# Summing the modulation over partitions with TensorE from the whole tile, at a later place in its order

## The chip, the cores and the metric

The kernel runs on one core of a Trainium2 chip. The metric is the time of one execution on the device in microseconds; less is better. PE is TensorE (matrix products), PEld its loading of weights, DVE VectorE, ACT ScalarE, POOL GpSimd, and SP SyncE, which issues the transfers.

## The reference, cut to what matters

Two blocks of two layers each, one sequence of 256 tokens of width 1024, all in fp32. The first block has a gated linear attention, an mLSTM and two mixtures of 16 experts. The second block is a transformer whose norms and residuals are modulated by a vector `c` (`ada`):

```
c_act = silu(c)                                    # 1 x 1024
for l in range(2):
    ada = c_act @ w_ada[l] + b_ada[l]              # 1 x 6144
    sh1, sc1, gt1, sh2, sc2, gt2 = split(ada, 6)
    h = rms(x, g_mix[l]) * (1 + sc1) + sh1
    ...                                            # two attentions, gates, mixed
    x = x + gt1 * (mixed @ w_out[l])
    h2 = rms(x, g_mlp[l]) * (1 + sc2) + sh2
    x = x + gt2 * (square(relu(h2 @ w_ff1[l])) @ w_ff2[l])
```

`ada` hangs on the input `c` alone, so it can be computed at any time before the norm that needs it. It is a product of one row with a 1024 x 6144 matrix for each layer.

## The kernel before

One program computes everything. Each engine has its own queue, worked in order; the order in which the program emits instructions is the order of every queue. The main line (dense products on PE) is emitted by plain functions (`dense`, `dense_T`, `out_proj`, `block_qk`), and after each step of it `B.tick()` lets the side jobs, written as generators, emit their next piece. A `Clock` keeps an estimated time for every engine and tile, from fixed costs; the choice between two engines (`AV`, `VG`, `VG2`) and the `calm` waits of side jobs go by these estimates. Weights of the dense products come as chunks of 128 x 1024 that are split into a high half (`hi`, by ACT or DVE) and a low half (`lo`, by DVE or POOL), two chunks ahead of their use.

`ada_cols` is the side job for `ada`. It takes the 12 column blocks j of 512 columns of each layer l, 24 blocks in all, (l, j), number n; each in four quarters q of 256 rows. A quarter is a transfer of 128 x 2 x 512, on ACT a product of its first half with a scalar per partition, and on DVE a product with the second half added. Quarters 1 to 3 are added to the tile of quarter 0, `acc`, by DVE or POOL. After the fourth, `acc` holds 128 x 512 terms still to be summed over the 128 partitions. Before the change DVE does the larger part of it: a transposition of all 32 x 32 squares, and a sum over 32 elements into `part` (128 x 4 x 4). PE finishes: four matmuls with 128 x 32 of `part` and the constant `c_fold` fold the four partition groups, each for its own 32 of the 128 output partitions. A matmul of fp32 shows as two records in the trace.

PE's step is a hook. `hooks` is a list of functions that wait for a good place in PE's order: the start of each dense product, its middle where `drained` is set, and in `out_proj` each chunk while the modulation of the second norm isn't there. A hook is taken there if `bool(hooks)` says that its input is ready on the planner's clock. Where something needs the result at once, `ada_need` (before the first norm of a layer (l, 3), before the second (l, 9)) and `unhook` (while side jobs are drained) take it without asking. The sum goes into the first columns of the PSUM tile that the dense product will use next, and ACT or DVE copies it out as `raw`.

Three tiles of 128 x 512 (`ada_T`) hold the quarters; `ada_used` says which are taken. Block n has its accumulator in tile n mod 3. Block numbers from 4 on are paced by `start` along the weight chunks. While the experts' weights stream, free tiles of the three serve as room for them (`ada_room`).

Of the kernel before, what the change touches and what calls it, by code (L numbers as in the profile page):

```python
# [26 lines left out]
F32 = mybir.dt.float32  # L27
# [4 lines left out]
OP = mybir.AluOpType  # L32
AX = mybir.AxisListType

P = 128
# [192 lines left out]
def tile_model(ctx: ExitStack, tc: tile.TileContext, I, out, stages=None, h_in=None):  # L228
    nc = tc.nc
    clock = Clock()  # L230
    PE, V, A, G = [Timed(clock, e, n) for e, n in
                   ((nc.tensor, "PE"), (nc.vector, "V"), (nc.scalar, "A"), (nc.gpsimd, "G"))]
# [8 lines left out]
    const = ctx.enter_context(tc.tile_pool(name="const", bufs=1))  # L241
# [163 lines left out]
    def kp_view(W, r0, rows, n0, n):  # L405
        return W[r0:r0 + rows, n0:n0 + n].rearrange("(k p) n -> p k n", p=P)
# [146 lines left out]
    class Hooks:  # L553
# [5 lines left out]
        def __bool__(self):  # L559
            if not self.fs:  # L560
                return False
            t = clock.t
            return max(clock.last(self.fs[0][1], False), min(t["A"], t["V"]) - 0.6) < t["PE"]

        def append(self, f, ap):
            self.fs.append((f, clock.span(ap)))
# [4 lines left out]
    hooks = Hooks()  # L571
# [204 lines left out]
    def gla():  # L776
# [23 lines left out]
        def load_ng(nb):  # L800
            ngs[nb] = bcast_row(ph, I["gla_norm_g"][:, nb * 512:(nb + 1) * 512], "row", 512)
        load_ng(0)
        small_loads()
        glr = early.tile([17, T], F32, name="glr")
        S.pump()
# [177 lines left out]
        if "l0" in stages:  # L983
            B.push(ada_cols(), side=True)
# [854 lines left out]
    ada_T, ada_used = [], {}  # L1839
# [8 lines left out]
    def ada_cols():  # L1848

        todo = [(l, j, q) for l in range(2) if f"l{l}" in stages for j in range(12) for q in range(4)]  # L1850
        ws = {}

        def load(i):
            if i < len(todo) and i not in ws and not ada_stop:
                l, j, q = todo[i]
                ada_open[0] += 1
                w = clock.slot("ada_w", 2, ada.tile([P, 2, 512], F32, name="ada_w", tag="ada_w", bufs=2))
                SP.dma_start(w, kp_view(I["w_ada_2"][l], q * 256, 256, j * 512, 512))
                ws[i] = w

        first = {g: next((i for i, (u, _) in enumerate(S.chunks) if S.units[u][3] == g), 0) for g in ("l0", "l1")}
        NB = (4, 10, 16, 22, 24)
        CB = [first["l0"] - 30, first["l0"] + 36, first["l1"] - 24, first["l1"] + 40, first["l1"] + 90]

        def start(x):
            i = max(j for j in range(4) if x >= NB[j])
            return CB[i] + (CB[i + 1] - CB[i]) * (x - NB[i]) / (NB[i + 1] - NB[i])

        load(0)
        load(1)  # L1870
        yield 14
        ada_T.extend(ada.tile([P, 512], F32, name="ada_t", tag=tag, bufs=n) for tag, n in
              (("ada_acc", 1), ("ada_t", 2), ("ada_t", 2)))
        acc = None
        for i, (l, j, q) in enumerate(todo):
            n = i // 4
            ada_at[0] = lambda: (load(i), load(i + 1))
            while i not in ws:
                load(i)
                load(i + 1)  # L1880
                yield 6 if i in ws else 1
            while n >= 4 and S.chunk_at < start(n + q / 4):
                yield
            while q == 1 and len(hooks.fs) > 1:
                yield
            w = ws[i]
            ada_used[n, q] = (n + (0, 2, 1, 2)[q]) % 3
            t = ada_T[ada_used[n, q]]
            if n >= 4:
                yield from calm("A", w)  # L1890
            A.activation(t, w[:, 0], AF.Copy, scale=ccol[:, 2 * q:2 * q + 1])
            if n >= 4:
                yield from calm("V", t)
            else:
                yield
            V.scalar_tensor_tensor(t, w[:, 1], ccol[:, 2 * q + 1:2 * q + 2], t, op0=OP.mult, op1=OP.add)
            ada_open[0] -= 1
            load(i + 2)
            if q:
                if n >= 4:  # L1900
                    yield from calm("G", t)
                else:
                    yield 1
                VG2.tensor_tensor(acc, acc, t, op=OP.add)
                if q < 3:
                    del ada_used[n, q]
            else:
                acc = t
                if n < 4:
                    yield 1  # L1910
            if q < 3:
                yield
                continue
            if n >= 4:
                yield from calm("V", acc)
            else:
                yield
            part = small.tile([P, 4, 4], F32, name="part", bufs=3)
            V.transpose(t, acc)
            if n >= 4:  # L1920
                yield from calm("V")
            V.tensor_reduce(part.rearrange("p k r -> p (k r)"), t.rearrange("p (b i) -> p b i", i=32), axis=AX.X,
                            op=OP.add)
            del ada_used[n, 0], ada_used[n, 3]

            def reduce(ps, l=l, j=j, part=part):
                for r in range(4):
                    PE.matmul(ps[32 * r:32 * r + 32, 0:4], c_fold, part[:, :, r], start=True, stop=True,
                              skip_group_check=True)
                k = slice(4 * j, 4 * j + 4)  # L1930
                raw = small.tile([P, 4], F32, name="raw", bufs=2)
                AV.copy(raw, ps[:, 0:4])
                VG2.tensor_tensor(adac[:, l, k], raw, bada[:, l, k], op=OP.add)
                if j % 6 == 3:

                    w = j // 6
                    V.tensor_copy(mod[:, l, w, 1], adac[:, l, 24 * w:24 * w + 8])
                    V.scalar_tensor_tensor(mod[:, l, w, 0], adac[:, l, 24 * w + 8:24 * w + 16], 1.0,
                                           gcol[:, l * 2 + w], op0=OP.add, op1=OP.mult)
                ada_done.add((l, j))  # L1940
            hooks.append(reduce, part)
            yield

    def calm(e, *aps):
        for _ in range(10):
            t = max([clock.t[e]] + [clock.last(clock.span(a), False, e) for a in aps])
            if t <= clock.t["PE"] + 0.9:
                return
            yield
# [472 lines left out]
    c_ident = ident  # L2422
# [7 lines left out]
                SP.dma_start(h[a * 64:a * 64 + 64, mt], rows[2 * mt + a])  # L2430
    n_kept = _OFFS[4][0]
    cst = const.tile([P, n_kept - P], F32, name="cst")
    c_fold = const.tile([P, 32], F32, name="fold")
    c_ones, c_iota, c_earl = [cst[:, o - P:o - P + n] for o, n in _OFFS[1:4]]
    mhalf = const.tile([P, 16], F32, name="mhalf")
    G.memset(mhalf, -0.5)
# [20 lines left out]

    def small_loads():
        ld = SP.dma_start
        V.tensor_reduce(c_fold, c_ident.rearrange("p (b m) -> p m b", m=32), axis=AX.X, op=OP.add)  # L2460
        ld(cst, I["cst"][:, P:n_kept])
        ld(rwg[:, 0], I["router_w"].rearrange("(k p) n -> p k n", p=P))
        for a, n in enumerate(("ln_g", "ln_b")):
            ld(lnpk[:, a], I[n][:, 0].rearrange("l (p k) -> p l k", k=8))
        ld(gatew, I["mlstm_w_in"][0][:, 4096:4104].rearrange("(k p) n -> p k n", p=P))
        for a in range(2):
            ld(bg[32 * a:32 * a + 4], I["mlstm_b_gates"][0, 4 * a:4 * a + 4].unsqueeze(1))
        ld(crow[0:64], I["mlstm_conv_w"][0].rearrange("j (f p) -> (j f) p", p=P))
        ld(crow[64:80], I["mlstm_conv_b"][0].rearrange("(f p) -> f p", p=P))
        ld(cb16.rearrange("p a b -> p (a b)"), I["cst"][:, _OFFS[4][0]:_OFFS[4][0] + 2 * P])  # L2470
# [82 lines left out]
    small = ctx.enter_context(sm_cm)  # L2553
# [21 lines left out]
    if first:  # L2575
        with tc.tile_pool(name="ring_b", bufs=RB) as rb, tc.tile_pool(name="rt", bufs=1) as rp, \
# [3 lines left out]
            if "gla" not in stages:  # L2580
                S.pump()
                small_loads()
# [6 lines left out]
            for i, s in enumerate(first):  # L2589
                nxt = (first + second)[i + 1] if i + 1 < len(first + second) else None  # L2590
                with tc.tile_pool(name="ph_" + s, bufs=1) as ph:
# [8 lines left out]
                    else:  # L2600
                        l = int(s[-1])
# [20 lines left out]
    else:  # L2622
        S.pump()
        small_loads()
        for _ in setup():
            pass
        B.push(ada_cols(), side=True)
    if second and not first:
        xin = rms_in(int(second[0][1]), 0)
# [34 lines left out]
```

## Time and profile before

| | |
|---|---|
| Time, median of 3 runs (lowest to highest) | 1734.81 us (1733.33 to 1739.93) |
| The profiled execution: time / span | 1734.7 us / 1732.9 us |
| Mean granted clock of TensorE | 0.953 |
| Instructions | 22647 |
| Busy: PE / PEld / DVE / ACT / POOL | 91% / 66% / 64% / 33% / 23% |
| Read from HBM | 419.77 MB, 243 GB/s over the span |

The span is the time from the first to the last instruction of the profiled execution. The second block's first layer begins near 845 us; its attention takes until about 1100, its MLP until about 1300, and the second layer the rest. The MLP of the first layer is where most of the second layer's modulation is computed. An idle time is put down to the event that ended it.

### The profile page before, as it was taken

The page shows a single profiled execution, that of the slowest core. Times are in us where ns is not written, and L with a number is a line of the kernel's source. Part 1 is how long each engine was busy: PE and PEld are TensorE (multiplying, and loading weights), DVE is VectorE, ACT ScalarE, POOL GpSimd, SP SyncE. Part 2 cuts the span into 40 slices and gives each one's busy share as a digit, 9 for nine tenths or more (in the row PEclk, how much of TensorE's full clock was granted, in tenths as well). Part 3 has the DMA queues.
Part 4 walks back from the last instruction along what each step waited for, and adds up shares of the span by engine and source line. Part 5 has one row for each costly group of instructions (what it writes and reads, how often), then busy time and mean ns, then how long its engine had stood idle before and what let it go on. Part 6 is the DMA issues. An engine that isn't in the chain of part 4 may idle for free.

```text
span 1732.9 us, 22647 instructions
## 1 busy us (share of the span) xinstructions
PE 1576.5 (91%) x8772; PEld 1136.3 (66%) x8774; DVE 1112.8 (64%) x1728; ACT 574.2 (33%) x973; POOL 395.3 (23%) x256
## 2 busy tenths in 40 slices
PE   7998999898998799989788998888998889989997
PEld 5865444336776544433466897778986679878996
DVE  4876113106887611121498979898889987779875
ACT  5223111105543211201344453533434544352210
POOL 1232000001333100000364324432125531222110
PEclk9998999898999899999998999999998999999999
DMA  9746999999755589999653676577764446547651
GB/s 321 284 149 229 360 392 411 391 360 238 240 190 194 198 322 373 409 406 387 208 179 110 196 202 221 171 250 257 250 240 152 158 138 179 191 137 241 194 180 41
DMA packets 165770, 422.43 MB, mean 244 GB/s; under 512 B 13017, under 2 KB 14193, under 8 KB 154642
## 3 DMA queue, kind: packets, MB, share of 16 engines
q1 hardware_dynamic: 165458, 420.75, 69.7%
q8 instruction: 73, 1.20, 0.3%
q14 instruction: 47, 0.39, 0.1%
q0 software_dynamic: 192, 0.10, 0.0%
HBM read 419.77 MB, written 1.05 MB: 243 GB/s over the span
## 4 chain that ended last, share of the span: by engine, by line
PE 27%; DVE 12%; issue 6%; ACT 2%; POOL 2%; DMA 1%; DVEq 0%; POOLq 0%; ACTq 0%
PE mm L175 16%; PE acc L175 7%; DVE ada_t L175 3%; DVE lo L175 2%; POOL lo L175 2%; PE sb L175 1%; DVE xs L175 1%; DMA ada_w<-in_w_ada 1%; DVE ro L175 1%; DVE rt L175 1%; ACT pa L175 1%; ACT hi L175 1%; DVE h L175 1%; DVE mx L175 1%; DVE hss L175 1%
## 5 line engine op out<-in xcount | busy, mean ns | idle before, releaser
L175 POOL TENSOR_TENSOR lo<-w,hi 128x1024 fp32r<-128x1024 f32 x104 | 264.4, 2548 | 505.7 <-ACT hi L175 495.9
L175 DVE TENSOR_TENSOR lo<-w,hi 128x1024 fp32r<-128x1024 f32 x204 | 261.4, 1287 | 21.2 <-ACT hi L175 15.3
L175 ACT CAST hi<-w 128x1024 fp32r<-128x1024 f32 x207 | 214.6, 1050 | 146.9 <-PE mm L175 99.9
L175 PE MATMUL mm<-hi,X_H 128*128 128x512 f32 x512 | 221.1, 432 | 29.8 <-ACT X_H L175 15.6
L175 PE MATMUL mm<-lo,X_H 128*128 128x512 f32 x512 | 210.5, 411 | 3.5 <-DVE lo L175 3.2
L175 PE MATMUL mm<-X_H,hi 128*128 128x256 f32 x704 | 206.0, 293 | 1.6 <-ACT raw L175 1.1
L175 PE MATMUL mm<-hi,X_L 128*128 128x512 f32 x512 | 197.4, 409 | 4.8 <-DVE X_L L175 4.7
L175 PE MATMUL mm<-X_L,hi 128*128 128x256 f32 x704 | 201.5, 286 | 0.0
L175 PE MATMUL mm<-X_H,lo 128*128 128x256 f32 x704 | 201.3, 286 | 0.0
L175 PE MATMUL up<-w,X 128*64 128x512 f32 x672 | 194.0, 599 | 0.8 <-ACT X L175 0.8
L175 PEld LDWEIGHTS mm<-hi,X_H 128*128 128x128 f32 x512 | 102.7, 201 | 61.5 <-issue 21.2
L175 PEld LDWEIGHTS mm<-X_H,hi 128*128 128x128 f32 x704 | 136.8, 194 | 4.0 <-ACT raw L175 1.3
L175 PEld LDWEIGHTS mm<-X_L,hi 128*128 128x128 f32 x704 | 137.0, 195 | 0.4
L175 PEld LDWEIGHTS mm<-X_H,lo 128*128 128x128 f32 x704 | 136.8, 194 | 0.0
L175 DVE SCALAR_TENSOR_TENSOR y<-dn,gsl,y 128x512 fp32r<-128x512 f32 x32 | 24.0, 751 | 162.0 <-ACT y L175 162.0
L175 POOL TENSOR_TENSOR ln_rs<-ln_rs,mhalf 128x1 f32<-128x1 f32 x8 | 4.9, 614 | 515.5 <-DVE ln_rs L175 515.5
L175 PEld LDWEIGHTS up<-w,X 128*64 128x64 f32 x672 | 58.7, 138 | 96.8 <-issue 93.0
L175 PEld LDWEIGHTS mm<-hi,X_L 128*128 128x128 f32 x512 | 100.7, 198 | 31.3 <-DVE X_L L175 8.5
L175 PEld LDWEIGHTS mm<-lo,X_H 128*128 128x128 f32 x512 | 102.8, 201 | 24.8 <-DVE lo L175 5.8
L175 PE MATMUL up<-wh,X 128*64 128x512 f32 x336 | 116.2, 604 | 0.0
L175 PE MATMUL dn<-w,hTt 128*64 128x512 f32 x336 | 105.3, 631 | 2.1 <-ACT hTt L175 2.1
L175 DVE TENSOR_TENSOR hb<-sa,up 128x512 f32<-128x512 f32 x16 | 11.0, 687 | 141.1 <-PE up L175 141.1
(412 smaller groups left out, 2953.2 us busy)
## 6 DMA issues: line engine op xcount, KB each, us to landing
w<-in_moe_w SPq DMA_DIRECT2D x126, 1024.0 KB, 9.8
w<-in_w_ff SPq DMA_DIRECT2D x64, 1024.0 KB, 5.5
wh<-in_moe_w SPq DMA_DIRECT2D x124, 512.0 KB, 11.5
ada_w<-in_w_ada SPq DMA_DIRECT2D x96, 512.0 KB, 4.2
w<-in_w_in SPq DMA_DIRECT2D x40, 1024.0 KB, 5.5
w<-in_mlstm_w_in SPq DMA_DIRECT2D x16, 1024.0 KB, 19.9
w<-in_gla_w_in SPq DMA_DIRECT2D x12, 1024.0 KB, 9.8
w<-in_w_out SPq DMA_DIRECT2D x8, 1024.0 KB, 6.1
```

What stands on the lines that cost most here:

```text
L175: r = f(*args, **kw)
```

## The change

DVE's transposition and sum go, with `part` and `c_fold`. PE sums each 128 x 128 quarter of `acc` over the partitions itself: the tile's columns are the weights, a column of ones moves, and the result is one column of 128 for each of the four. So four matmuls with 128 x 128 weights replace four with 128 x 32. The hook is taken at a place where the tile has been ready for 5 us on the planner's clock, unless it is taken without asking. `acc` stays taken until PE's sum is emitted; so the tiles of the quarters are dealt out in another order, and a wait of the job changes: before, the second quarter waited while more than one hook was open, now the third waits until the block before it has been summed.

```
-            return max(clock.last(self.fs[0][1], False), min(t["A"], t["V"]) - 0.6) < t["PE"]
+            return max(clock.last(self.fs[0][1], False) + 5.0, min(t["A"], t["V"]) - 0.6) < t["PE"]
...
-            while q == 1 and len(hooks.fs) > 1:
+            while (n - 1, 0) in ada_used and q == 2:
                 yield
             w = ws[i]
-            ada_used[n, q] = (n + (0, 2, 1, 2)[q]) % 3
+            ada_used[n, q] = (n + (0, 1, 2, 1)[q]) % 3
...
-            part = small.tile([P, 4, 4], F32, name="part", bufs=3)
-            V.transpose(t, acc)
-            if n >= 4:
-                yield from calm("V")
-            V.tensor_reduce(part.rearrange("p k r -> p (k r)"), t.rearrange("p (b i) -> p b i", i=32), axis=AX.X,
-                            op=OP.add)
-            del ada_used[n, 0], ada_used[n, 3]
-
-            def reduce(ps, l=l, j=j, part=part):
-                for r in range(4):
-                    PE.matmul(ps[32 * r:32 * r + 32, 0:4], c_fold, part[:, :, r], start=True, stop=True,
+            del ada_used[n, 3]
+
+            def reduce(ps, l=l, j=j, n=n, acc=acc):
+                for f in range(4):
+                    PE.matmul(ps[:, f:f + 1], acc[:, f * P:(f + 1) * P], c_ones[:, 0:1], start=True, stop=True,
                               skip_group_check=True)
+                del ada_used[n, 0]
...
-            hooks.append(reduce, part)
+            hooks.append(reduce, acc)
...
-    c_fold = const.tile([P, 32], F32, name="fold")
...
-        V.tensor_reduce(c_fold, c_ident.rearrange("p (b m) -> p m b", m=32), axis=AX.X, op=OP.add)
```

## Rows read from the trace of the kernel before

**Rows 1.** The page, busy time, share of the span and instructions of each engine.

```profile
PE 1576.5 (91%) x8772; PEld 1136.3 (66%) x8774; DVE 1112.8 (64%) x1728; ACT 574.2 (33%) x973; POOL 395.3 (23%) x256
```

**Rows 2.** Busy time by stretch: us, busy us of PE, PEld, DVE, ACT, POOL, PEclk, DMA share.

```profile
845.00:1100.00 255.00, 218.04 (x1336) 183.25 (x1338) 221.79 (x361) 115.99 (x234) 108.98 (x75) 0.93 0.55 176
1100.00:1205.00 105.00, 94.18 (x611) 85.34 (x610) 93.15 (x102) 46.41 (x68) 34.59 (x13) 0.93 0.74 249
1205.00:1300.00 95.00, 92.92 (x564) 81.79 (x562) 83.47 (x96) 36.23 (x48) 20.73 (x9) 1.00 0.71 240
```

**Rows 3.** Tile views of ada_t and part: duration ns min/median/max, first and last start us.

```profile
L175 DVE STREAM_TRANSPOSE ada_t<-ada_t x24: 696/711/715, 98.9 to 1620.5; 128x512 f32<-128x512 f32 x24
...
L175 DVE TENSOR_REDUCE part<-ada_t x24: 677/686/689, 99.7 to 1621.3; 128x16 f32<-128x512 f32 x24
```

**Rows 4.** Order of time on PE around one reduction: start us, us, what.

```profile
977.90 0.28 PE L175 MATMUL mm<-X_H,lo 128*128 128x256 f32 x1
978.11 0.25 PE L175 MATMUL mm<-part,fold 128*32 128x4 f32 x8
978.29 0.39 PE L175 MATMUL mm<-X_H,hi 128*128 128x256 f32 x1
978.51 0.28 PE L175 MATMUL mm<-X_L,hi 128*128 128x256 f32 x1
```

**Rows 5.** Order of time on PE, narrow matmuls with a full weight tile.

```profile
34.30 0.39 PE L175 MATMUL mm<-lo,X_H 128*128 128x512 f32 x1
34.52 1.84 PE L175 MATMUL dps<-cg,rg 128*128 128x4 f32 x16
36.23 0.47 PE L175 MATMUL mm<-hi,X_H 128*128 128x512 f32 x1
36.54 0.39 PE L175 MATMUL mm<-lo,X_H 128*128 128x512 f32 x1
```

**Rows 6.** Order of time on PE, the same weight width with 128 columns moving.

```profile
1261.61 1.95 PE L175 MATMUL adar<-ident,adac 128*128 128x128 f32 x16
1263.49 0.25 PE L175 MATMUL mm<-part,fold 128*32 128x4 f32 x8
```

**Rows 7.** Order of time on PE: the four reductions with an idle time before them.

```profile
532.16 0.25 PE L175 MATMUL bgp<-part,fold 128*32 128x4 f32 x8 [3.22 <-DVE part L175]
...
1139.23 0.24 PE L175 MATMUL bgp<-part,fold 128*32 128x4 f32 x8 [2.02 <-DVE part L175]
...
1160.69 0.28 PE L175 MATMUL mm<-part,fold 128*32 128x4 f32 x8 [4.27 <-DVE part L175]
...
1196.49 0.29 PE L175 MATMUL bgp<-part,fold 128*32 128x4 f32 x8 [3.45 <-DVE part L175]
```

**Rows 8.** Busy time by stretch behind two of these (PEclk is the granted clock).

```profile
1160.70:1165.20 4.50, 4.50 (x28) 4.48 (x29) 3.94 (x6) 1.82 (x3) 0.78 (x1) 0.50 1.03 382
...
1196.50:1202.90 6.40, 6.40 (x37) 6.38 (x38) 3.02 (x4) 2.61 (x4) 0.00 (x0) 0.50 0.88 288
```

**Rows 9.** Order of time on DVE behind the third of these idle times.

```profile
1162.03 1.22 DVE L175 TENSOR_TENSOR lo<-w,hi 128x1024 fp32r<-128x1024 f32 x1
```

**Rows 10.** Order of time on DVE and PE: waits of PE behind a reduction.

```profile
880.84 0.69 DVE L175 TENSOR_REDUCE part<-ada_t 128x16 f32<-128x512 f32 x1
...
887.52 0.77 PE L175 MATMUL mm<-hi,X_H 128*128 128x512 f32 x1 [4.02 <-DVE xs L175]
...
1337.26 0.76 PE L175 MATMUL mm<-hi,X_H 128*128 128x512 f32 x1 [3.45 <-DVE xs L175]
```

**Rows 11.** Order of time on DVE, the last quarter of block (0, 9).

```profile
1067.36 0.75 DVE L175 SCALAR_TENSOR_TENSOR ada_t<-ada_w,ccol,ada_t 128x512 f32<-128x512 f32 x1
...
1069.15 2.89 DVE L175 TENSOR_TENSOR ada_t<-ada_t 128x512 f32<-128x512 f32 x1
```

**Rows 12.** Order of time on PE: the reductions of blocks (0, 8) and (0, 9).

```profile
1055.00 0.24 PE L175 MATMUL mm<-part,fold 128*32 128x4 f32 x8
...
1073.63 0.24 PE L175 MATMUL bgp<-part,fold 128*32 128x4 f32 x8
```

## Prediction, made before the result was known

> **What bounds the kernel now.** Read the page's busy times first [rows 1]: PE is busy for 91% of the span, DVE for 64%. So PE idles for 1732.9 - 1576.5 = 156.4 us in all, and whatever the change does must either add to PE's work or take from those 156 us. The changed sums run along the whole kernel but belong to the second block, so the stretches come next [rows 2]. In the first attention stretch (845 to 1100) DVE is busy for 221.8 of 255 us and PE for 218.0: both are near their limit, and PE often waits for DVE. In the first half of the MLP (1100 to 1205) DVE has 93.2 of 105 us, PE 94.2, at a granted clock of 0.93. From 1205 to 1300 PE has 92.9 of 95 us: there, work taken from DVE buys nothing and work given to PE is paid in full.
>
> Then the sums themselves. Each of the 24 column blocks ends with a transposition and a reduction on DVE, 0.71 and 0.69 us [rows 3], together 24 x 1.40 = 33.6 us. PE then folds in eight records (four matmuls, two passes each). Last, PE in order of time: four of the 24 folds have an idle time before them that ended with DVE's reduction: 3.22 + 2.02 + 4.27 + 3.45 = 12.96 us [rows 7]. Behind the third and the fourth PE runs 4.5 and 6.4 us at a granted clock of 0.50, which is the 1.2 GHz level, where it had been idle just before [rows 8]. The same work at 2.4 GHz would have taken about half of these 10.9 us, so up to 5.4 us; matmuls bound by other things halve less, and I take 5.0.
>
> **What the change costs on PE.** A fold now takes little, because its weight tiles are 32 columns wide: eight records within 0.18 us (978.11 to 978.29). What it delays is more: from the matmul before it to the second behind it 0.61 us pass (977.90 to 978.51) where two usual steps of 0.12 us would make 0.24 [rows 4], so 0.37 us. The new matmuls load 128 x 128 of the tile as weights and move one column. Nothing in the trace moves one column, but 16 records with full weights and 4 columns take 1.71 us (34.52 to 36.23), 0.107 each; from the matmul before to the second behind 2.24 us pass where two steps of 0.23 make 0.46, so 16 records delay by 1.78 [rows 5]. With 128 columns moving a record takes 1.88 / 16 = 0.117 us [rows 6]. From 128 columns to 4 the step falls only by a tenth, so the weights set it, and one column will not be cheaper to speak of. Eight records then cost 8 x 0.107 = 0.86 and delay by 0.86 + 0.07 = 0.93. The difference per block is 0.93 - 0.37 = 0.56 at the least, and 0.86 - 0.18 = 0.68 if the edges cost as much as the fold's; I take 0.60, or 24 x 0.60 = 14.4 us in all. The lower bound, should the loads hide, is nothing.
>
> Here a rule bears on the sum. Rows 5 show 0.107 us per narrow record [rows 5]. The Trainium skill, TensorE: Matmul & The Clock Gate, section Back-to-back issue gap, gives streams of matmuls with up to 64 columns a gap of about 25 ns, and by that the eight records would cost no more than the fold does; the section LDWEIGHTS of the same page lets a load take its columns divided by 1.2 in ns, 107 for 128 columns, and by that the sum stands as above. The trace agrees with the second for full weights, and with 0.18 / 8 = 0.023 us for narrow ones it is near the first. The first is a rival below.
>
> Not every block pays. In two places PE goes from the fold straight into a wait for DVE's xs: the idle time before 887.52 begins at 883.50, that before 1337.26 at 1333.81 [rows 10]. What PE does there longer lies within these 4.02 and 3.45 us. The fold at 1055.00 [rows 12] also comes shortly before a wait. So 21 x 0.60 = 12.6 us are exposed; bounds 10 (more blocks hidden, 18 x 0.56) and 16 (24 x 0.68).
>
> **What it gives back.** (1) The waits of the four folds. The hook is now taken only when the tile was finished 5 us ago on the planner's clock, and the tile is finished 1.40 us earlier than part was. The largest of the four waits, 4.27 us, is smaller than 6.4, so all four should go. At 532 I count the whole 3.22 us. The other three lie within 1100 to 1205 and are worth 2.02 + 4.27 + 3.45 = 9.74, with the slow clock 14.7 us, if nothing else becomes late. But DVE is nearly full there [rows 2]: five blocks fall into this stretch (three of them in [rows 7]) and take 5 x 1.40 = 7.0 from its 93.2 us, leaving 86.2. If DVE keeps its 11.9 us of idle time, because these are waits for ACT, PE and transfers, the stretch ends at 98.0, 7.0 us earlier; PE alone would allow 94.2 - 5.0 + 5 x 0.6 = 92.2, 12.8 earlier. What is late next is the low half of split weights: lo at 1162.03 to 1163.25 [rows 9] is needed two chunks behind the dense product that begins at 1160.9, and PE would come 2.02 + 4.27 and some 2 of the slow clock, 8 us, sooner against DVE's 2.8 from the two blocks before it. I take the DVE end: 7.0 net of PE's added 3.0, so 10.0 before that cost. Bounds 4 (only DVE's own shortening is passed on, half of it) and 14.7.
>
> (2) Where PE waits for DVE soon after a transposition. At 880.84 the reduction ends 6 us before PE gets its xs, and the same pattern stands at 1337.26 [rows 10]: DVE's queue is in order, so 1.40 us less ahead of xs is 1.40 us less wait. Two places make 2.8 us; bounds 0 (POOL or ACT is late instead) and 4.2 (a third such place). The other transpositions lie where PE is full or DVE has room, and give nothing.
>
> (3) The fold matrix made once at the start lies beside the first loads: 0.
>
> **The added wait.** Three tiles serve as a ring. The accumulator was free after the transposition; now it is held until PE's sum has been issued, and the third quarter of the next block waits for that. Blocks cannot overtake any more. Where blocks follow each other slowly this costs nothing. It is tight at block (0, 9), which has to be done before the second norm: PE takes it at 1073.63 [rows 12], 1.6 us after the last addition ended (1069.15 + 2.89) [rows 11]. If it isn't taken there, 18 more matmuls of 0.23 us follow before it is forced, at 1077.8. In the changed order block (0, 8), read at 1055.00, must be read first; one place later would be in the out projection's second dense product, about 1062.6, and then two quarters follow of 4.7 us each (1067.36 to 1072.04, [rows 11]): 1072. That still holds, so I count 0; another slip would not hold.
>
> **The sum.** 12.6 - 3.2 - 10.0 - 2.8 = -3.4 us against the profiled execution's 1734.7 (span 1732.9 and 1.8 around it), which is within 0.1 us of the median of the runs, 1734.81: **1731.3 us**.
>
> **Rivals.**
> A, PE is the only bound in the MLP: all 14.7 us come free, and a third place of (2): 12.6 - 3.2 - 14.7 - 4.2 = -9.5, 1725.2. For it: PE has 92% of its time in that stretch as soon as the waits are gone, and DVE can run ahead by several chunks. Against it: DVE was 90% busy with its waits already counted.
> B, the ring is too tight: the third quarter starts a place late twice, at block (0, 9) and at its like in the second layer. From the start at 1073.6 two quarters end at 1083.0, 5.2 us behind the forced place, and PE then runs on at the low clock for some 5 us, 2.5 more: 7.7 per time, 15.4 in all. -3.4 + 15.4 = +12.0, 1746.7. It decides from about 12 us on, that is when both are late. For it: 1.6 us of room before, and a 5 us delay added. Against it: the forced place is 4 us later, and side work goes on during the projection.
> C, DVE's lag stays and PE only waits for lo instead of part (or a forced hook, which doesn't ask for the 5 us, stalls as before, so that the later place does nothing): of the 14.7 us 4 come back, (2) gives nothing: 12.6 - 3.2 - 4 = +5.4, 1740.1. With 16 for PE it is +8.8, at the edge of slower.
> D, the weight loads hide and the sums cost no more than folds: -16.0, 1718.7. Rows 5 speak against it [rows 5].
>
> **How the numbers follow.** A run of this kernel is told from another from about 0.5% on, 8.7 us: 1726.1 and 1743.5 are the edges. Chances: forecast 0.37 (its own range 1727 to 1737), A 0.29, D 0.03, C 0.16, B 0.15. A and D are faster (0.32); the forecast and two thirds of C are the same (0.48); B and the rest of C are slower (0.20). The range from 1720 to 1746 leaves out D, the best of A with PE's cost at 10, and the worse half of B.
>
> **What would show it.** Right: no transposition and no part on DVE, its busy time lower by about 33; the 192 matmuls with one column at 0.107 us a step, eight in 0.86; no idle time of PE behind these loads; no stretch at 0.50 between 1160 and 1203. Wrong: steps near 0.025 (D); new waits of PE for lo or fl between 1130 and 1205 of the old time (C); idle time before the first matmul of a sum that ended with ada_t, or a gap before the norm at 1080 (B). The planner reads its own clocks, so less work on DVE also moves splits between DVE, ACT and POOL; if the tables of these engines' work differ by more than the removed instructions, some of the difference is from there and the terms above don't hold it.

## The result and the profile after

The changed kernel takes 1760.98 us (median, 1758.18 to 1761.96) against 1734.38 for the kernel before beside it: a ratio of 1.0141, interval 1.0122 to 1.016, or 26.6 us more. The forecast was 1731.3 in a range of 1720 to 1746: the time lies outside it, on the slower side.

First the busy times of the page, and of the view of PE's waits the lines that concern the change (what PE ran next, what it waited for: us in total, times, longest).

```profile
PE 1592.3 (91%) x8772; PEld 1151.6 (66%) x8774; DVE 1100.0 (63%) x1685; ACT 570.7 (32%) x970; POOL 389.4 (22%) x253
```

```profile
PE mm L175 <- DVE lo L175: 13.3, 13, 2.5
PE bgp L175 <- DVE ada_t L175: 12.6, 2, 11.4
...
PE kv L175 <- DVE og L175: 6.6, 3, 3.7
```

The first of these lines in the kernel before:

```profile
PE mm L175 <- DVE lo L175: 3.2, 5, 1.0
```

Against [rows 1] PE has 15.8 us more to do. DVE has only 12.8 less, although 33.6 us of transpositions and sums went [rows 3]: the planner gave it five more `lo` splits (204 before, 209 now), and some of its instructions take longer beside POOL (six of 28 casts into `fh` 2.5 us in place of 0.43). The four waits for `part` [rows 7] are gone. In their place stand two for `ada_t`, one of them 11.4 us long, and PE's waits for `lo` before a `mm` have grown from 3.2 to 13.3 us.

PE in order of time, changed kernel: the first sums of layer 0 but block (0, 0), with what stands around two of them.

```profile
483.63 1.05 PE L175 MATMUL cv<-cst,ada_t 128*128 128x1 f32 x8
...
509.51 1.45 PE L175 MATMUL kv<-vx,mixed 64*128 64x257 f32 x4 [3.70 <-DVE og L175]
...
511.41 0.63 PE L175 MATMUL mm<-lo,X_H 128*128 128x512 f32 x1
511.84 0.63 PE L175 MATMUL mm<-hi,X_L 128*128 128x512 f32 x1
...
525.24 1.83 PE L175 MATMUL bgp<-cst,ada_t 128*128 128x1 f32 x8 [3.66 <-DVE mixed L175]
...
561.75 1.05 PE L175 MATMUL bgp<-cst,ada_t 128*128 128x1 f32 x8
...
969.85 0.39 PE L175 MATMUL mm<-hi,X_L 128*128 128x512 f32 x1
970.09 0.95 PE L175 MATMUL mm<-cst,ada_t 128*128 128x1 f32 x8
970.89 0.37 PE L175 MATMUL mm<-X_H,hi 128*128 128x256 f32 x1
971.10 0.28 PE L175 MATMUL mm<-X_L,hi 128*128 128x256 f32 x1
...
1058.24 1.05 PE L175 MATMUL mm<-cst,ada_t 128*128 128x1 f32 x8 [0.25 <-DVE th L175]
...
1082.99 1.05 PE L175 MATMUL bgp<-cst,ada_t 128*128 128x1 f32 x8 [1.16 <-DVE ada_t L175]
1095.45 1.87 PE L175 MATMUL bgp<-cst,ada_t 128*128 128x1 f32 x8 [11.40 <-DVE ada_t L175]
```

Count the blocks. The sums at 483.63, 525.24, 561.75 and 970.09 are (0, 1) to (0, 4); those at 1058.24, 1082.99 and 1095.45 are (0, 7) to (0, 9). In the kernel before (0, 8) is read at 1055.00 and (0, 9) at 1073.63 [rows 12]. So at the norm that needs (0, 9), the changed kernel is a whole block behind. What PE waits for in those 11.4 us is seen on DVE and ACT, in order of time.

```profile
1085.66 0.75 DVE L175 SCALAR_TENSOR_TENSOR ada_t<-ada_w,ccol,ada_t 128x512 f32<-128x512 f32 x1 [1.13 <-ACT ada_t L175]
1088.60 0.75 DVE L175 SCALAR_TENSOR_TENSOR ada_t<-ada_w,ccol,ada_t 128x512 f32<-128x512 f32 x1 [2.18 <-ACT ada_t L175]
1089.38 0.69 DVE L175 TENSOR_TENSOR ada_t<-ada_t 128x512 f32<-128x512 f32 x1
1090.90 0.75 DVE L175 SCALAR_TENSOR_TENSOR ada_t<-ada_w,ccol,ada_t 128x512 f32<-128x512 f32 x1 [0.83 <-ACT ada_t L175]
1091.69 0.69 DVE L175 TENSOR_TENSOR ada_t<-ada_t 128x512 f32<-128x512 f32 x1
1093.91 0.75 DVE L175 SCALAR_TENSOR_TENSOR ada_t<-ada_w,ccol,ada_t 128x512 f32<-128x512 f32 x1 [1.53 <-ACT ada_t L175]
1094.70 0.69 DVE L175 TENSOR_TENSOR ada_t<-ada_t 128x512 f32<-128x512 f32 x1
```

```profile
1087.84 0.72 ACT L175 ACTIVATE ada_t<-ada_w,ccol 128x512 f32<-128x512 f32 x1 [2.21 <-DMA ada_w<-in_w_ada]
1090.15 0.72 ACT L175 ACTIVATE ada_t<-ada_w,ccol 128x512 f32<-128x512 f32 x1 [1.59 <-DMA ada_w<-in_w_ada]
1093.16 0.72 ACT L175 ACTIVATE ada_t<-ada_w,ccol 128x512 f32<-128x512 f32 x1 [2.29 <-DMA ada_w<-in_w_ada]
```

All four quarters of block (0, 9) reach DVE after the sum at 1082.99, about 2.75 us apart, and the last three each wait for their transfer, then for ACT, then for DVE. Nothing of this is beside work of PE.

The mLSTM loses as well. In the order of time on DVE and POOL:

```profile
503.80 2.33 DVE L175 SCALAR_TENSOR_TENSOR hn_rs<-hn_rs,den 128x2 f32<-128x2 f32 x1 [0.83 <-POOL hn_rs L175]
506.06 2.91 DVE L175 SCALAR_TENSOR_TENSOR ada_t<-ada_w,ccol,ada_t 128x512 f32<-128x512 f32 x1
508.89 0.47 DVE L175 SCALAR_TENSOR_TENSOR og<-o,hn_mv,og 128x256 f32<-128x256 f32 x1
```

```profile
503.73 4.69 POOL L175 TENSOR_TENSOR lo<-w,hi 128x1024 fp32r<-128x1024 f32 x2
```

A quarter of the side job that usually takes 0.75 us takes 2.91 here, while POOL runs two splits, and `og`, which PE's product `kv` needs, stands behind it. PE idles 3.70 us. The second idle time, 3.66 us, belongs to the sum at 525.24 itself: it is taken in the middle of a product, where a hook needs one PSUM tile more (`bgp`), and the profile puts its wait down to `mixed`, by which DVE reads the earlier `cv` out of such tiles. At the start of a product, a sum shares the product's own tile. Behind each of these idle times, and behind the 11.4 us, the granted clock is low (windows: length, busy us of PE, PEld, DVE, ACT, POOL, then the clock):

```profile
509.50:514.40 4.90, 4.78 (x13) 3.34 (x13) 4.79 (x12) 1.66 (x2) 0.00 (x0) 0.65 0.89 308
525.20:531.00 5.80, 5.76 (x18) 4.93 (x19) 5.29 (x10) 2.77 (x5) 0.42 (x3) 0.50 0.34 93
1095.40:1101.50 6.10, 6.05 (x18) 5.18 (x19) 2.29 (x8) 2.56 (x4) 1.30 (x2) 0.50 0.52 144
```

The table takes the same matmul (the k-th of its kind) in two traces and subtracts its start in the kernel before. It holds the changed kernel and four of the experiments below, each from its profiled execution. Free tiles were profiled in their fastest execution (1715.83 us, median 1722.7), so that column stands some 7 us too low against the others near the end; steps within a column are safer to read than gaps between columns.

| us in the kernel before | place | changed | narrow, held | free tiles | wait early | wait late |
|---|---|---|---|---|---|---|
| 507 | mLSTM | -1.6 | -1.8 | -5.2 | -4.3 | -2.1 |
| 523 | mLSTM | +11.3 | +10.4 | -4.8 | +11.9 | -1.6 |
| 888 | attention, layer 0 | +4.5 | +4.2 | -6.5 | +5.1 | -3.1 |
| 1072 | out projection | +2.4 | +5.1 | -9.1 | 0.0 | -4.4 |
| 1091 | behind the second norm | +17.8 | +24.2 | -7.8 | +11.0 | +1.4 |
| 1132 | MLP | +18.2 | +24.9 | -6.7 | +11.4 | +1.9 |
| 1216 | MLP | +11.4 | +17.0 | -14.5 | +6.1 | -5.6 |
| 1264 | MLP | +18.4 | +23.8 | -13.7 | +6.9 | -2.0 |
| 1391 | attention, layer 1 | +15.0 | +25.6 | -17.9 | +4.7 | -1.3 |
| 1532 | behind its out projection | +23.2 | +33.9 | -18.8 | +3.8 | +7.1 |
| 1709 | near the end | +23.1 | +33.2 | -18.9 | +3.8 | +6.9 |

The changed kernel falls back in four steps: 12.9 us in the mLSTM, 15.4 between 1072 and 1091, 7.0 between 1216 and 1264, 8.2 between 1391 and 1532. In between it gains. In the third step lie two of the waits for `lo`:

```profile
1236.28 0.39 PE L175 MATMUL mm<-X_H,lo 128*128 128x256 f32 x1 [2.52 <-DVE lo L175]
...
1262.62 0.38 PE L175 MATMUL mm<-X_H,lo 128*128 128x256 f32 x1 [2.52 <-DVE lo L175]
```

### The profile page after: what moved, and what is told of

Its sections match the earlier page's. It is cut to its first block, busy times and chain, and to the rows that moved or that the text cites. A ratio compares the mean times of both kernels' runs of the same rounds, so it can differ in the third digit from the quotient of the medians.

```text
span 1756.4 us, 22580 instructions
## 1 busy us (share of the span) xinstructions
PE 1592.3 (91%) x8772; PEld 1151.6 (66%) x8774; DVE 1100.0 (63%) x1685; ACT 570.7 (32%) x970; POOL 389.4 (22%) x253
## 4 chain that ended last, share of the span: by engine, by line
PE 25%; DVE 15%; issue 5%; ACT 2%; DMA 2%; POOL 1%; DVEq 0%; ACTq 0%; POOLq 0%; SPq 0%
PE mm L175 15%; PE acc L175 6%; DVE ada_t L175 3%; DMA ada_w<-in_w_ada 2%; DVE lo L175 2%; PE sb L175 1%; DVE xs L175 1%; ACT pa L175 1%; DVE th L175 1%; DVE hi L175 1%; DVE rt L175 1%; DVE h L175 1%; DVE fh L175 1%; DVE ro L175 1%; DVE X_L L175 1%
## 5 line engine op out<-in xcount | busy, mean ns | idle before, releaser
L175 POOL TENSOR_TENSOR lo<-w,hi 128x1024 fp32r<-128x1024 f32 x99 | 258.0, 2616 | 475.1 <-ACT hi L175 470.1
L175 DVE TENSOR_TENSOR lo<-w,hi 128x1024 fp32r<-128x1024 f32 x209 | 270.5, 1300 | 18.4 <-ACT hi L175 12.6
L175 PEld LDWEIGHTS mm<-hi,X_H 128*128 128x128 f32 x512 | 102.7, 201 | 52.4 <-issue 14.4
L175 DVE SCALAR_TENSOR_TENSOR ada_t<-ada_w,ccol,ada_t 128x512 f32<-128x512 f32 x96 | 97.4, 1016 | 31.1 <-ACT ada_t L175 31.0
L175 ACT ACTIVATE ada_t<-ada_w,ccol 128x512 f32<-128x512 f32 x96 | 69.6, 725 | 129.0 <-DMA ada_w<-in_w_ada 107.3
L175 PE MATMUL up<-wh,X 128*64 128x512 f32 x320 | 108.9, 603 | 0.0
```

What stands on the lines that cost most here:

```text
L175: r = f(*args, **kw)
```

## The experiments

Theory: the held accumulator costs the time. Only one block may be unsummed, so a block can't begin its third quarter before the one ahead of it has found its place on PE. Rivals: PE's wider sums, the 5 us, and the changed load of DVE. Each ratio is to the kernel before, run beside it, with its 95% interval; 0.001 is 1.7 us. A difference of two ratios from different groups of runs is uncertain by 0.002 to 0.004, some 4 to 7 us.

**The 5 us taken away from the change.**

```
-    return max(clock.last(self.fs[0][1], False) + 5.0, min(t["A"], t["V"]) - 0.6) < t["PE"]
+    return max(clock.last(self.fs[0][1], False) + 0.0, min(t["A"], t["V"]) - 0.6) < t["PE"]
```

> The changed kernel with the 5 us of the hook's condition set to 0; the sums stay whole-tile sums. Ring theory (an accumulator is held until PE's sum, so a late sum makes the next block late, and the forced place before the second norm of the first layer waits 11.4 us): sums come earlier, so part of this wait goes; 1745 to 1755 us. Place theory (the later place itself is bad, by taking places in the middle of products and delaying blocks): all of it goes but the price on PE; 1738 to 1746. Price theory (24 times 0.6 us of PE is the loss, the rest is noise of the planner): no gain, 1758 to 1768, since waits of PE for the tile come back.

1760.29 us, 1.0139 (1.0103 to 1.0174): no change. The 5 us don't make the loss. The ring theory's 1745 to 1755 missed, and the price theory's 1758 to 1768 was met, so by itself this run speaks for the price of the sums; the next two kernels decide against it.

**Free tiles, the 5 us kept.** Any free tile serves, and one block more may be unsummed.

```
-            while (n - 1, 0) in ada_used and q == 2:
+            while (n - 2, 0) in ada_used and q == 1:
                 yield
...
-            ada_used[n, q] = (n + (0, 1, 2, 1)[q]) % 3
+            ada_used[n, q] = min((i for i in range(3) if i not in ada_used.values()), key=ada_last.get)
+            ada_last[ada_used[n, q]] = (n, q)
```

> The changed kernel with the same three tiles, but each quarter takes any tile that is free, so two summed-up blocks may wait for PE instead of one; the 5 us stay. Ring theory: the wait of 11.4 us before the second norm goes, 1742 to 1750 us, and the sum of block (0, 9) is ready well before its forced place. Place theory and price theory: within 4 us of the changed kernel, 1757 to 1765.

1722.7 us, 0.9939 (0.9921 to 0.9956): faster than the kernel before, and 35 us (0.0202) under the change. The ring theory has the direction right, but the gain is larger than its 1742 to 1750. PE has no wait for `ada_t`, and its sums come as early as this:

```profile
503.30 1.05 PE L175 MATMUL mm<-cst,ada_t 128*128 128x1 f32 x8
539.64 1.05 PE L175 MATMUL mm<-cst,ada_t 128*128 128x1 f32 x8
877.76 0.95 PE L175 MATMUL mm<-cst,ada_t 128*128 128x1 f32 x8
...
1069.44 0.95 PE L175 MATMUL bgp<-cst,ada_t 128*128 128x1 f32 x8
```

Block (0, 4) is summed at 877.76 in place of 970.09, block (0, 9) at 1069.44 without idle time.

**The kernel before with the hold alone:** narrow folds and DVE's work kept, no 5 us, but tiles, wait and hold of the change.

```
-            while q == 1 and len(hooks.fs) > 1:
+            while (n - 1, 0) in ada_used and q == 2:
...
-            ada_used[n, q] = (n + (0, 2, 1, 2)[q]) % 3
+            ada_used[n, q] = (n + (0, 1, 2, 1)[q]) % 3
...
-            del ada_used[n, 0], ada_used[n, 3]
+            del ada_used[n, 3]
...                                            # in reduce, behind the fold
+                del ada_used[n, 0]
```

> The kernel before with the ring of the changed one alone: tiles dealt out as there, the accumulator held until PE's narrow fold is issued, the third quarter waiting for that; transposition and reduction stay on DVE, no 5 us. If holding one accumulator is the loss by itself: +20 to +40 us, 1754 to 1774, with waits before forced places. If it only bites together with the wide sums or the 5 us: within 5 us, 1730 to 1740.

1769.6 us, 1.0207 (1.0182 to 1.0233): 36 us slower than the kernel before, in the same places as the change (table, "narrow, held"). Its sums of (0, 8) and (0, 9), PE in order of time:

```profile
1089.77 0.29 PE L175 MATMUL bgp<-part,fold 128*32 128x4 f32 x8 [6.46 <-DVE part L175]
...
1102.07 0.29 PE L175 MATMUL bgp<-part,fold 128*32 128x4 f32 x8 [12.01 <-DVE part L175]
```

So letting only one block be unsummed costs 36 us put in and 35 taken out, whatever the sums look like. With free tiles the accumulator is still held until PE's sum; what went there is the wait for the block before.

**Wait or tile order?** The changed kernel's wait, with any free tile.

```
             while (n - 1, 0) in ada_used and q == 2:
...
-            ada_used[n, q] = (n + (0, 1, 2, 1)[q]) % 3
+            ada_used[n, q] = min((i for i in range(3) if i not in ada_used.values()), key=ada_last.get)
+            ada_last[ada_used[n, q]] = (n, q)
```

> The changed kernel with its wait for the block before (third quarter), but any free tile. If the wait is what costs, the time is that of the change within 5 us, 1756 to 1766, with PE's long idle time before the sum of block (0, 9). If the fixed dealing of the tiles costs, the time falls to near 1722.

1760.2 us, 1.0149 (1.0124 to 1.0175): as slow as the change, with 12.65 us of idle time before block (0, 9). The wait is what costs, not the fixed order of the tiles.

**The wait for early blocks alone, and for late ones alone** (free tiles in both).

```
+            while (n < 6 and (n - 1, 0) in ada_used and q == 2) or ((n - 2, 0) in ada_used and q == 1):
...                                            # the other kernel: n >= 6
```

> The wait for the block before holds for blocks below 6 alone, later ones may have one unsummed block ahead of them. If the loss in the mLSTM (about 9.6 us in the changed kernel's trace) is one of its own, the time is 1722 + 10 = about 1732. If it is only carried along, or made up for in the attention behind it, near 1722.

> The wait for the block before holds from block 6 on. If the two places are independent and the out projections cost 15 + 8 us and what hangs on them, the time is 1722 + 23 to 28 = 1745 to 1750, with PE's idle time of 9 to 12 us before the sum of block (0, 9). If the early lag is what makes block (0, 9) late, near 1722 without that idle time.

Early: 1736.92 us, 1.002 (1.0002 to 1.0038). Late: 1741.66 us, 1.0047 (1.0026 to 1.0068). Over the mean of two runs of free tiles (0.9939 and, below, 0.9921) that is 0.009 and 0.0117, or 16 and 20 us; together 36 (each uncertain by some 4), of the 0.0211, 37 us, by which the change stands above free tiles. Both times lie outside what was expected, the early one above 1732, the late one between its two cases. The two differ in where block (0, 4) is summed. PE, wait early, then wait late:

```profile
525.60 1.43 PE L175 MATMUL bgp<-cst,ada_t 128*128 128x1 f32 x8 [3.67 <-DVE mixed L175]
562.37 1.05 PE L175 MATMUL bgp<-cst,ada_t 128*128 128x1 f32 x8
971.45 0.95 PE L175 MATMUL mm<-cst,ada_t 128*128 128x1 f32 x8
...
1088.74 1.44 PE L175 MATMUL bgp<-cst,ada_t 128*128 128x1 f32 x8 [4.39 <-DVE ada_t L175]
```

```profile
506.50 1.05 PE L175 MATMUL mm<-cst,ada_t 128*128 128x1 f32 x8
542.89 1.66 PE L175 MATMUL mm<-cst,ada_t 128*128 128x1 f32 x8
881.07 0.95 PE L175 MATMUL mm<-cst,ada_t 128*128 128x1 f32 x8
...
1078.34 1.26 PE L175 MATMUL bgp<-cst,ada_t 128*128 128x1 f32 x8 [3.87 <-DVE ada_t L175]
```

With the wait early, the mLSTM's loss is there in full (table, 507 to 523: 16.2 us) and block (0, 4) slips to 971.45; with the wait late the mLSTM loses 0.5 us there, and (0, 4) is at 881.07. Either alone leaves about 4 us of idle time before (0, 9), far below the 9 to 12 that were expected of the late one; both together leave 11.4. So the long wait at the norm comes from the early lag and the late wait together. In the second layer it is the late wait that makes the step (table, 1391 to 1532: 8.4 us with it, none with the early one). Against free tiles the late wait loses little by little: 4.7 us at 1072, 9.2 at 1091, 16.6 at 1391, 25.9 at 1532, in the profiled executions; 3.1 of it stand at 507 already, before that wait holds for any block, and belong to the two executions.

**The later place alone,** in the kernel before.

```
-    return max(clock.last(self.fs[0][1], False), min(t["A"], t["V"]) - 0.6) < t["PE"]
+    return max(clock.last(self.fs[0][1], False) + 5.0, min(t["A"], t["V"]) - 0.6) < t["PE"]
```

> The kernel before with 5 us added to the hook's condition and nothing else: transposition, reduction on DVE and narrow folds stay, and no accumulator is held. Ring theory: the four waits of folds (12.96 us) go and nothing holds the blocks back, 1722 to 1732 us. Place theory: late places alone cost, 1740 to 1752. Price theory: no difference or a small gain, 1728 to 1736.

1724.85 us, 0.9944 (0.9924 to 0.9964): the later place alone is worth 9.5 us there.

**The width of the sums alone.** The kernel before, each fold preceded in its group by four matmuls of the wide form, whose result nobody reads and which wait for nothing that DVE makes; once as it was and once with the 5 us.

```
             def reduce(ps, l=l, j=j, part=part):
+                for f in range(4):
+                    nc.tensor.matmul(ps[:, 4 + f:5 + f], c_ident, c_ones[:, 0:1], start=True, stop=True,
+                                     skip_group_check=True)
```

> The kernel before with four more matmuls in each of the 24 folds, 128 x 128 weights (the identity) and one column moving, into columns of the same PSUM tile that nobody reads; the planner isn't told of them, so every engine's order stays. This is the price of the wide sums alone. Price theory: 24 x 0.86, less the blocks that hide it, +14 to +20 us, 1748 to 1754. Ring and place theories: mostly the same, since this was a term of the forecast (12.6 for a difference of 0.60): +12 to +20; under +6 would say that PE has room behind the folds and that the whole loss is order.

> The kernel before with the 5 us (1724.9) and, as in the run with four unread wide matmuls in each fold, the price of the wide sums; order of every engine as without them. If PE has the same room as there: +8, 1733. If it was the folds' own waits that hid part of the price, and these are gone now: +14 to +20, 1739 to 1745.

Without the 5 us 1742.43 us, 1.0041 (1.002 to 1.0061), 8 us more than before; with them 1742.69 us, 17.8 more than the later place alone. PE's earlier waits had hidden the other half: where PE is going to wait for `part`, the extra matmuls run in that time. Its waits for `part`, and those of `mm` for `xs`, fall from 20.5 us in the kernel before to 13.3 with the extra matmuls. The first time (+8) was in neither of the expected ranges (+12 to +20, or under +6), the second was in its +14 to +20.

**DVE's work put back.** Free tiles, and the transposition and the sum into `part` as before, `part` unread.

```
+            part = small.tile([P, 4, 4], F32, name="part", bufs=3)
+            V.transpose(t, acc)
...
+            V.tensor_reduce(part.rearrange("p k r -> p (k r)"), t.rearrange("p (b i) -> p b i", i=32), axis=AX.X,
+                            op=OP.add)
```

> Whole-tile sums with freely chosen tiles and the 5 us (1722.7), and DVE does transposition and reduction as before into a tile nobody reads. This prices the 33.6 us of DVE. If the relief of DVE is worth what PE pays (8) and 2 more: 1731 to 1735. If it is worth nothing off the bound: 1721 to 1726, and then the wide sums would be all but free.

1734.16 us, 1.0006 (0.999 to 1.0022): DVE's relief is worth 11.5 us once the tiles are free.

**Free tiles and the 5 us.** First none, then beside each other none and 5 (both kernels a second time) and 2.5.

```
-    return max(clock.last(self.fs[0][1], False) + 5.0, min(t["A"], t["V"]) - 0.6) < t["PE"]
+    return max(clock.last(self.fs[0][1], False) + 0.0, min(t["A"], t["V"]) - 0.6) < t["PE"]
...                                            # the other kernels: + 5.0, + 2.5
```

> Whole-tile sums with freely chosen tiles (1722.7) and the 5 us set to 0. If the later place is worth by itself what it was in the kernel before (9.5 us): 1730 to 1735, with PE waiting for the tile at some sums. If the tile is early enough without transposition and reduction: 1720 to 1726, no such waits.

> The kernel with any free tile and no 5 us of margin, timed a second time. If the margin itself costs time, its ratio to the kernel before stays about 0.988 to 0.989 and it stands some 10 us under the kernel with the margin in the same call (1713 against 1723). If the difference between the two earlier runs came from the chip that each ran on, the two now lie within 3 us.

> The kernel with any free tile and the 5 us of margin, timed beside the one without it. Margin theory: about 1723, ratio 0.994. Rival (the chip): within 3 us of the kernel without the margin, whichever of the two values both take.

> Free tiles with 2.5 us of margin. If the margin costs in proportion, because it moves hooks to later places, the time lies between 1713 and 1723, near 1718. If only a few places of PE's order decide it, it takes one of the two values, 1713 or 1723, within 3 us.

The first gave 1713.12 us, 0.9885 (0.9851 to 0.9918), below both of its expected ranges, which looked like 10 us for the 5 us. Side by side it was 1718.09 (0.9899, 0.9881 to 0.9917) without them, 1721.25 (0.9921, 0.9905 to 0.9936) with them, and 1720.22 (0.9925, 0.9904 to 0.9946) with 2.5. The difference is 3 us, within the intervals. With free tiles the 5 us can't be told from none.

**The wide sum in narrow pieces.** Free tiles, no 5 us, the same sums from sixteen matmuls with 32 columns of weights.

```
                 for f in range(4):
-                    PE.matmul(ps[:, f:f + 1], acc[:, f * P:(f + 1) * P], c_ones[:, 0:1], start=True, stop=True,
-                              skip_group_check=True)
+                    for r in range(4):
+                        (nc.tensor, PE)[r == 3].matmul(
+                            ps[32 * r:32 * r + 32, f:f + 1], acc[:, f * P + 32 * r:f * P + 32 * r + 32],
+                            c_ones[:, 0:1], start=True, stop=True, skip_group_check=True)
```

> Free tiles, no margin, and each wide sum (four matmuls with 128 columns of weights) given as sixteen matmuls with 32 columns of weights in the four column groups: the same sums, 32 records in the place of 8. If the price of the wide sum is the load of 128 columns of weights for one moving column, and narrow weights load beside each other at the fold's 0.022 us a record, a sum takes 32 x 0.022 = 0.7 us against 0.86, and the 24 sums save 3 to 4 us: about 1709. If sixteen narrow loads run one behind another, at the wide record's 0.107, a sum takes over 3 us and the kernel is some 60 us slower. Rival that the length of the sum is no cost at all: 1713 within 3 us.

1712.02 us, 0.9873 (0.9856 to 0.989), the fastest version here, 6.1 us under the same kernel with wide sums beside it. The two intervals overlap a little (0.9881 to 0.989), the earlier run of that kernel gave 0.9885, and 1712 us lies within the rival's 1713 as well, so the gain isn't certain. PE in order of time around one sum, the first and last of its 32 records:

```profile
502.44 0.20 PE L1924 MATMUL mm<-cst,ada_t 128*32 128x1 f32 x3
...
502.70 0.17 PE L175 MATMUL mm<-cst,ada_t 128*32 128x1 f32 x1
502.80 0.50 PE L175 MATMUL mm<-hi,X_H 128*128 128x512 f32 x1
```

The 32 records take 0.36 us (502.44 to 502.80), where the 0.7 expected assumed 0.022 each and 8 wide ones take 0.80 (970.09 to 970.89). Per block that is about 0.44 to 0.5 us, over 24 blocks 11; 6 of it is seen in the time at most.

## Why the prediction was wrong

**The step that failed** is "The added wait", with its "That still holds, so I count 0". The term is 36 us, measured both ways. The mechanism was named, as rival B, and mis-sized there too, at 15.4. It was priced as a start that comes one place late at block (0, 9) and its like. Three things were missing. The lag doesn't begin at (0, 9): it begins with block (0, 2), summed at 525.24 where the kernel before has a sum at 508.77, and is handed from block to block; (0, 3) follows at 561.75 instead of 532.16. The first two quarters of (0, 4), which DVE works in the mLSTM in the kernel before (from 531.93 to 539.25), then come only behind it, from 883.14 on, and its sum moves from 883.26 to 970.09. The prediction says that the wait costs nothing where blocks follow each other slowly; but in the mLSTM the lag moves a quarter in front of `og` on DVE's queue and the sum of (0, 2) into the middle of a product; these are the two waits of 3.7 us, each with a stretch at a low clock behind it. And at the norm all four quarters were missing, not two. The sign that the prediction names for B, idle time before the first matmul of a sum that ended with `ada_t`, is there: 11.40 us at 1095.45. The sums of (0, 2) and (0, 4) in the kernel before, PE in order of time:

```profile
508.77 0.24 PE L175 MATMUL mm<-part,fold 128*32 128x4 f32 x8
...
883.26 0.24 PE L175 MATMUL mm<-part,fold 128*32 128x4 f32 x8
```

**PE's sums** (12.6, bounds 10 and 16) were nearly right. A record takes 0.80 / 8 = 0.100 us against the 0.107 forecast. The added wide matmuls cost 17.8; the folds that they replace cost 21 x 0.37 = 7.8 by the prediction's own figure, so net 10.0, the lower bound. Directly, the kernel with DVE's work put back, which has wide sums and free tiles, takes 9.3 us more than the later place alone, which has folds (1734.16 - 1724.85). That loads would hide (rival D) is refuted. The Trainium skill, TensorE: Matmul & The Clock Gate, section LDWEIGHTS, lets a load of 128 columns take 107 ns; the trace's 0.100 agrees to within a tenth. The Trainium skill's gap of about 25 ns, which the prediction takes from the section Back-to-back issue gap of that page, counts no loads, as the section says; here each record has its own (eight of either kind for each sum).

**The later place and DVE's relief** (3.2 + 10.0 + 2.8 = 16.0) were too small: 9.5 and 11.5, each measured in one kernel of its own, are 21.0. All four waits for `part` went, as forecast. The 6.8 us gained from 1132 to 1216 look like the forecast 7.0 net, but the kernel with the hold and DVE's full load gains 7.9 there as well, so this gain is no sign of the 7.0 us of DVE's work that the forecast built on. What was called late next, `lo`, is: two waits of 2.52 us, at 1236 and 1262, stand in the step that loses 7.0 behind it. Where DVE's relief arises is read as in the table: the kernel with DVE's work put back lags behind free tiles by 1.6 us at 888, 6.7 at 1105, 9.0 at 1205, 13.7 at 1300 and 14.4 at 1340, and by hardly more at 1709 (15.4; the two profiled executions are 15.6 apart, the medians 11.5). Between 1105 and 1205, where the forecast put its largest gain, it grows by 2.3; between 1205 and 1300, where the prediction says that work taken from DVE buys nothing, by 4.7.

**The sum with the measured terms:** 10.0 - 9.5 - 11.5 = -11.0 without the wait, against -11.7 and -13.2 measured for free tiles with the 5 us (1722.7 - 1734.39, 1721.25 - 1734.41). With 36 for the wait it is +25.0, against +26.6. The terms are uncertain by 3 to 5 us each, so that an agreement within 3 is partly luck. They also follow one path: first the 5 us, then the wide sums, then DVE's work taken away. In another order the shares are others, for with free tiles no worth of the 5 us is seen (1718.09 without them, 1721.25 with them). With the wait loosened by one block the time is nearer to rival A's 1725.2 than to the forecast, and the change is faster.

**The range.** The prediction says that 1720 to 1746 leaves out the best of A with PE's cost at 10. By its own terms that is 10 - 3.2 - 14.7 - 4.2 = -12.1, or 1722.6, which lies inside.

## What to carry to other kernels

A buffer that is freed one step later is priced over the whole chain of its users, not at the one place where it is tightest: follow the release from the first block on, and ask at each whether the next one still meets its place. A side job held to one unfinished item can fall a whole item behind and then runs with nothing beside it at the first forced use. If a tile must be held longer, let one more item be open; here a fixed rotation of the tiles had to go for that, and it turned 1.4% slower into 0.6% to 0.8% faster. Dropping the rotation and keeping the wait changed nothing (1760.2 us).

## What the runs showed of the hardware that was not expected

Narrow weights took less than the kernel before showed: 32 records with 128 x 32 weights and one moving column took 0.36 us, 0.011 each, where the folds' eight took 0.18, or 0.022 each. The folds move four columns, and a cost that comes once for each group would also weigh more on eight records than on 32; no run separates these. In the changed kernel a DVE product with a scalar and addition (`scalar_tensor_tensor`) of 128 x 512 took 2.91 us in place of 0.75, and one of 128 x 2 took 2.33 in place of 0.16, each beginning while POOL ran a split of 128 x 1024 and ending about when that split did (0.6 us behind it at most). The kernel before has such a case too (128 x 2 in 2.37 us, at 517.88). Not every instruction is held up: the six into `mixed`, which read PSUM, took 2.93 us beside such a split (520.16 in the kernel before) and 2.94 with POOL idle (512.62 in the changed one).
